# Two-layer attention backbone on Trainium2: reading gated attention back without its last pair, cutting the first output quarter inside the last attention unit, and adding residuals to partial sums

## The chip, the cores and the metric

The kernel runs on one core of a Trainium2 chip (trn2). The metric is device time in microseconds (us) of one execution, as the median of several runs. Beside it there is a hardware profile of one execution. Its engines are PE (TensorE matmul), PEld (weight load of TensorE), DVE (VectorE), ACT (ScalarE), POOL (GpSimd) and SP, the queue that issues nearly all DMAs.

## The reference

Two layers over 1024 latent tokens and 256 context tokens, width 1024. Layer 0 is windowed attention; the change lies wholly in the end of layer 1, multi-head latent attention, whose context output is not needed:

```
def attend(qn, qr, kn, kr, v):
    s = (einsum("bqhd,bkhd->bhqk", qn, kn) + einsum("bqhd,bkd->bhqk", qr, kr)) * scale
    p = softmax(s, axis=-1)
    return einsum("bhqk,bkhd->bqhd", p, v)
...
yx = (ox * silu(gx)) @ w_out                 # ox: 1024 tokens x 1024 channels, 16 heads of 64
x = x + gate_x[:, None] * yx                 # gate_x is folded into w_out by the kernel
return rms_norm(x, final_g)                  # y / sqrt(mean(y*y) + eps) * final_g
```

## The kernel before

**Attention.** The 16 heads are 8 pairs; each pair's 1024 queries are two halves of 512. That makes 16 units (`UnitB`), number `ui` = 2 * pair + half. A unit goes over `NT` = 10 chunks of 128 keys: `score` (L1820) makes the scores of two heads on PE, `exp` (L1830) takes their exponentials on ACT, an engine adds them up for the softmax's denominator (L1834 and L1836: POOL, but DVE in unit 15), and `PV` (L1843) multiplies by the values on PE, its result always in bank 7 of PSUM. `top` (L1786, L1792) finds the next unit's row maxima, `turn` and `shift` (L1800, L1804) bring them into its scores. `fin` (L1847) copies the PV result out and loads the gate; `fin2` (L1854, L1856) sums the denominator on PE and copies it out on ACT; `inv` (L1860, DVE) takes the reciprocal of a half of 256 tokens; `gate` (two POOL multiplications L1865 and a store L1867) writes gated attention to `og_d`, [pair, channel, token], in HBM. Units 0 to 13 are gated in chunk 0 of the unit two later; unit 14 inside unit 15 from chunk 5 on; unit 15 after the attention is over.

**Free PE slots.** After unit `ui`, PE makes the keys of the next pair (`make_K`) or, after units 3, 7 and 11, the values of the next four heads (`make_V`, five PSUM tiles in three banks, each copied out by ACT at L1732).

**The output weight** is multiplied by the gate and combined to seven 512x512 blocks of four k-slices each by `wo_pieces`, a generator that `wo_step` advances a few steps per unit, on POOL or on DVE. Every block is kept as two parts (a rounded `hi` on ACT and a rest `lo`, `split`, L281 and L282; on POOL L1880 and L1881). 18 of the 28 slices are written to `wb_d` in HBM and later read back by `wo_back` (L1886).

**The output product** (`out_sets`) takes 256 tokens at a time: four sets n = 0 to 3. The set's tokens are two rows of 128, its channels two halves, so it is a 2x2 block matrix a11, a12 / a21, a22; the 2x2 product takes seven block products instead of eight, in the order `WAY`: a11 with B11, a12 with B21, s2 with T2, s1 with T1, s4 with B22, s3 with T3, a22 with T4, where s1 = a21+a22, s2 = s1-a11, s4 = a12-s2, s3 = a11-a21. One block product is 12 matmuls (L286, L287, L288: hi by hi, lo by hi, hi by lo, for four k-slices). `fetch_raw(n)` loads the set's two rows from `og_d`, all eight pairs (a11 and a21 are pairs 0 to 3; a12 and a22 pairs 4 to 7; pair 7 is the last to come: sets 0 and 1 need unit 14, sets 2 and 3 unit 15). `sums` makes s1 to s4 on POOL; `all_cuts` splits the seven operands into hi and lo in a ring of six; five operands are ready ahead of the product.

After the products DVE adds up `ya` (row 0) and `yb` (row 1) from PSUM, POOL adds the residual rows `xa`, `xb`, ACT sums the squares (`square`, L2020), `tile_rstd` makes the norm's factor on POOL, `tile_out` scales and stores. For set 3 the last product, a22 with T4, is done in two halves of 256 columns.

**Order.** In this part each engine works its instructions off in the order of the code, and so does each DMA queue: an SP DMA that waits holds back all those behind it. Names in the profile: `arena_r` and `arena_f` are the two big buffers in which nearly everything lies, `PB` is PSUM, `small` holds the columns of the norm.

Of the kernel before, what the change touches and what calls it, by code (L numbers as in the profile page):

```python
# [11 lines left out]
F32 = mybir.dt.float32  # L12
# [205 lines left out]
def kernel(ctx: ExitStack, tc: tile.TileContext, t, out, dbg=None):  # L218
# [1739 lines left out]
    def fetch_raw(n):  # L1958
        for j in range(2):
            ts = slice((2 * n + j) * 128, (2 * n + j) * 128 + 128)  # L1960
            load(out=rawr[n % 2][j].bitcast(F32), in_=og_d[:, :, ts].rearrange("c p n -> p c n"))
# [16 lines left out]
    def sums(n):  # L1978
        (a11, a12), (a21, a22) = raw_parts(n)
        P = nc.gpsimd  # L1980
        ss[n] = s1, s2, s3, s4 = [shp(sr1.next(), 4, 128) for _ in range(4)]
        P.tensor_add(s1, a21, a22)
        yield
        P.tensor_sub(s2, s1, a11)
        yield
        P.tensor_sub(s4, a12, s2)
        yield
        P.tensor_sub(s3, a11, a21)
        yield

    def all_cuts():
        for n in range(4):
            (a11, a12), (a21, a22) = raw_parts(n)
            yield cut(a11, nc.vector if n else nc.gpsimd)
            yield cut(a12, nc.vector if n else nc.gpsimd)
            s1, s2, s3, s4 = ss[n]
# [25 lines left out]
    def out_sets(A, made, xs, u):  # L2022
# [7 lines left out]
        for n in range(4):  # L2030
# [4 lines left out]
            plus = sums(n + 1) if n < 3 else iter(())  # L2035
            for j in range(6 if last else 7):
                g = 7 * n + j
                ps = out_product(A.pop(0), WAY[j])
                if j < 4:
                    next(plus, None)  # L2040
# [5 lines left out]
                if n == 0 and j == 0:  # L2046
                    u.fin2(psd)
                if n == 0 and j < 2:
                    u.inv(j)
                    u.gate(256 * j, 256 * j + 256)  # L2050
                if n == 0 and j == 1:
                    wo_back("T4", 3)
# [14 lines left out]
                if j == 3:  # L2067
                    p5, u4 = ps, ur.next()
                    V.tensor_add(u4, ps, u2)
                if j == 4:  # L2070
                    V.tensor_add(ya[:, up], ps, u4)
                    at(g + 1, lambda ya=ya, xa=xa: P.tensor_add(ya[:, up], ya[:, up], xa[:, up]))
                    at(g + 1 if last else g + 2, lambda ya=ya, sa=sa: (square(ya, up, sa, 1), tile_rstd(sa)))
                    if not last:
                        for c in range(2):
                            at(g + 3, lambda ti=2 * n, ya=ya, sa=sa, c=c: tile_out(ti, ya, sa, c))
                if j == 5:
# [3 lines left out]
                    if last:  # L2081
                        V.tensor_add(yb[:, up], yb[:, up], xb[:, up])
                        P.tensor_add(u3, u3, xb[:, lo])
                        square(yb, up, sb, 1)
                        continue
# [11 lines left out]
        z = ur.next()  # L2097
        halves = [slice(256 * h, 256 * h + 256) for h in range(2)]
        for h, cs in enumerate(halves):
            ps = out_product(W, "T4", cs)  # L2100
            V.tensor_sub(yb[:, cs], u3[:, cs], ps)
            square(yb, cs, sb, 2 if h else 0)
            if h == 0:
                V.tensor_mul(z, yb[:, up], fg[:, up])
# [188 lines left out]
```

## Time and profile before

| what | value |
|---|---|
| median of 3 runs | 1485.5 us (1485.28 to 1487.9) |
| profiled execution | 1484.49 us, its span 1482.7 us |
| PE busy | 1454.4 us, 98% of the span |
| DVE, POOL, ACT busy | 76%, 59%, 50% |
| chain that ended last | PE 87%, DVE 5%, issue 2%, DMA 2%, ACT 2%, POOL 1% |
| granted clock of PE | 0.999 |

How to read it: the shares are means over stages that differ, so the end of the program is shown by stage. The work from the profile's 1260 us to its end, by stage (busy us of each engine, number of instructions, then clock, DMA share and GB/s; the stages are unit 11's end, units 12 to 14, unit 15, the output product, the end):

```profile
1260.00:1291.00 31.00, 30.08 (x222) 22.66 (x220) 24.76 (x26) 12.92 (x17) 30.15 (x16) 1.00 0.30 98
1291.00:1369.00 78.00, 78.00 (x570) 54.50 (x566) 53.91 (x76) 33.49 (x38) 74.33 (x37) 1.00 0.40 139
1369.00:1400.00 31.00, 27.16 (x163) 14.64 (x161) 21.65 (x16) 15.93 (x21) 18.56 (x13) 1.00 0.59 188
1400.00:1474.00 74.00, 73.61 (x335) 61.32 (x335) 57.37 (x61) 24.77 (x56) 57.41 (x57) 1.00 0.45 157
1474.00:1483.00 9.00, 0.05 (x1) 0.00 (x0) 3.78 (x9) 1.92 (x7) 1.05 (x2) 0.77 0.31 117
```

The columns are length, then PE, PEld, DVE, ACT and POOL. Times in the text, such as "at 1391.95", are us from the span's start.

### The profile page before, as it was taken

The page shows a single profiled execution, that of the slowest core. Times are in us where ns is not written, and L with a number is a line of the kernel's source. Part 1 is how long each engine was busy: PE and PEld are TensorE (multiplying, and loading weights), DVE is VectorE, ACT ScalarE, POOL GpSimd, SP SyncE. Part 2 cuts the span into 40 slices and gives each one's busy share as a digit, 9 for nine tenths or more (in the row PEclk, how much of TensorE's full clock was granted, in tenths as well). Part 3 has the DMA queues.
Part 4 walks back from the last instruction along what each step waited for, and adds up shares of the span by engine and source line. Part 5 has one row for each costly group of instructions (what it writes and reads, how often), then busy time and mean ns, then how long its engine had stood idle before and what let it go on. Part 6 is the DMA issues. An engine that isn't in the chain of part 4 may idle for free.

```text
span 1482.7 us, 25146 instructions
## 1 busy us (share of the span) xinstructions
PE 1454.4 (98%) x8988; PEld 1176.6 (79%) x8988; DVE 1128.9 (76%) x2064; ACT 746.2 (50%) x1419; POOL 870.4 (59%) x765
## 2 busy tenths in 40 slices
PE   7999999999999999999999999999999999999897
PEld 4888888888888888889888888766777767775586
DVE  4787789648778888878988777677777687776776
ACT  4421222259888878877554433443444434443432
POOL 2463366256464444456300240699999999999685
PEclk9999999999999999999999999999999999999999
DMA  9555644573343333338344566021312332325652
GB/s 337 171 173 170 212 155 164 181 251 108 122 141 121 104 100 100 94 95 263 95 120 119 172 224 204 15 64 44 103 47 74 102 118 89 104 88 183 223 174 100
DMA packets 152150, 204.90 MB, mean 138 GB/s; under 512 B 13388, under 2 KB 101068, under 8 KB 152024
## 3 DMA queue, kind: packets, MB, share of 16 engines
q1 hardware_dynamic: 147048, 196.63, 41.3%
q10 hardware_dynamic: 4976, 6.66, 1.3%
q8 instruction: 71, 1.16, 0.3%
q14 instruction: 55, 0.45, 0.1%
HBM read 143.46 MB, written 55.59 MB: 134 GB/s over the span
## 4 chain that ended last, share of the span: by engine, by line
PE 87%; DVE 5%; issue 2%; DMA 2%; ACT 2%; POOL 1%; SPq 0%; ACTq 0%; POOLq 0%; DVEq 0%
PE PB L286 14%; PE PB L287 14%; PE PB L288 14%; PE PB L1820 12%; PE PB L1843 8%; PE PB L738 5%; PE PB L1786 5%; PE PB L728 5%; PE PB L699 3%; PE PB L698 2%; PE PB L912 1%; DVE arena_r L282 1%; PE PB L1854 1%; PE PB L883 1%; PE PB L917 1%
## 5 line engine op out<-in xcount | busy, mean ns | idle before, releaser
L286 PE MATMUL PB<-arena_r 128*128 128x512 f32 (+2 forms) x1180 | 432.7, 367 | 2.0 <-DVE arena_f L1262 1.1
L287 PE MATMUL PB<-arena_r 128*128 128x512 f32 (+2 forms) x1180 | 427.0, 362 | 3.8 <-POOL arena_r L282 3.7
L288 PE MATMUL PB<-arena_r 128*128 128x512 f32 (+2 forms) x1180 | 426.4, 362 | 0.0
L1836 POOL TENSOR_TENSOR arena_f<-arena_f 128x1024 f32<-128x1024 f32 x120 | 292.8, 2440 | 9.4
L286 PEld LDWEIGHTS PB<-arena_r 128*128 128x128 f32 x1180 | 222.5, 189 | 47.2 <-issue 10.7
L287 PEld LDWEIGHTS PB<-arena_r 128*128 128x128 f32 x1180 | 222.6, 189 | 35.7 <-POOL arena_r L282 5.2
L288 PEld LDWEIGHTS PB<-arena_r 128*128 128x128 f32 x1180 | 222.5, 189 | 33.2
L1820 PE MATMUL PB<-arena_r 64*128 64x512 f32 (+1 forms) x1600 | 227.0, 395 | 0.0
L1830 ACT ACTIVATE arena_f<-PB 128x1024 f32<-128x1024 f32 x160 | 164.6, 1028 | 119.5 <-PE PB L1820 91.6
L1792 DVE TENSOR_REDUCE krF<-PB 128x1 f32<-128x512 f32 (+1 forms) x264 | 166.9, 678 | 50.6 <-PE PB L1786 50.6
L1820 PEld LDWEIGHTS PB<-arena_r 64*128 64x128 f32 (+1 forms) x1600 | 175.7, 185 | 16.1 <-issue 5.2
L705 DVE CUSTOM_DVE_ANT_0 arena_f<-PB,arena_f,small 128x256 f32<-128x256 f32 (+1 forms) x288 | 148.2, 525 | 51.0 <-PE PB L699 32.8
L281 ACT CAST arena_r<-PB 128x512 fp32r<-128x512 f32 (+2 forms) x207 | 115.4, 564 | 107.0 <-PE PB L288 68.3
L281 ACT CAST arena_r<-arena_f 128x512 fp32r<-128x512 f32 (+1 forms) x156 | 90.8, 612 | 133.7 <-PE PB L288 33.8
L282 DVE TENSOR_TENSOR arena_r<-PB,arena_r 128x512 fp32r<-128x512 f32 (+2 forms) x207 | 134.3, 661 | 26.7 <-ACT arena_r L281 26.0
L1843 PE MATMUL PB<-arena_f 128*64 128x512 f32 x640 | 146.4, 595 | 0.5 <-ACT arena_f L1830 0.5
L282 POOL TENSOR_TENSOR arena_r<-arena_f,arena_r 128x512 fp32r<-128x512 f32 (+1 forms) x48 | 67.5, 1427 | 105.2 <-ACT arena_r L281 105.0
L711 ACT ACTIVATE arena_f<-arena_f,small 128x640 f32<-128x640 f32 (+2 forms) x160 | 119.1, 745 | 15.5 <-DVE small L705 13.9
L508 DVE SCALAR_TENSOR_TENSOR arena_f<-arena_f,small 128x512 f32<-128x512 f32 x98 | 114.0, 1208 | 11.7 <-DMA arena_f<-ada_w 11.5
L738 PE MATMUL PB<-arena_r 128*128 128x512 f32 x336 | 118.9, 430 | 0.2 <-DVE arena_r L282 0.2
L282 DVE TENSOR_TENSOR arena_r<-arena_f,arena_r 128x512 fp32r<-128x512 f32 (+1 forms) x108 | 91.6, 872 | 27.6 <-ACT arena_r L281 24.9
L1786 PE MATMUL PB<-arena_r 64*128 64x512 f32 (+1 forms) x768 | 111.7, 355 | 0.1
(244 smaller groups left out, 2247.0 us busy)
## 6 DMA issues: line engine op xcount, KB each, us to landing
arena_f<-ada_w SPq DMA_DIRECT2D x96, 256.0 KB, 4.0
arena_r<-q_d SPq DMA_DIRECT2D x160, 128.0 KB, 2.8
arena_f<-a_w_in SPq DMA_DIRECT2D x40, 256.0 KB, 3.4
arena_f<-x_d SPq DMA_DIRECT2D x18, 512.0 KB, 4.8
arena_f<-b_w_in SPq DMA_DIRECT2D x36, 256.0 KB, 3.1
wb_d<-arena_r SPq DMA_DIRECT2D x18, 512.0 KB, 2.9
arena_r<-wb_d SPq DMA_DIRECT2D x18, 512.0 KB, 9.2
arena_f<-x SPq DMA_DIRECT2D x16, 512.0 KB, 5.8
```

The lines of the kernel that those rows point to most:

```text
L281: nc.scalar.copy(hi, src)
L282: (lo_eng or nc.vector).tensor_sub(lo, src, hi.bitcast(F32))
L286: nc.tensor.matmul(o, ah, bh, start=first, stop=False)
L287: nc.tensor.matmul(o, al, bh, start=False, stop=False)
L288: nc.tensor.matmul(o, ah, bl, start=False, stop=last)
L738: nc.tensor.matmul(self.pv, V[:, self.chunks[ci], self.g, :], PT[:, s], start=ci == 0 and s == 0, stop=ci == self.m - 1 and s == 1,)
L1786: nc.tensor.matmul(bank[:, o : o + n], self.q[r, s, bs], k[r, 0, n0 : n0 + n], start=s == 0, stop=s == 2)
L1792: nc.vector.reduce_max(self.mxp[:, e, b : b + 1, i], bank[:, 0:n], AX.X)
L1820: nc.tensor.matmul(PB[:, b + e, :], k[r, s, cs], q[r, sq], start=i == 0, stop=i == 4)
L1830: nc.scalar.activation(E, PB[:, b : b + 2, :], AF.Exp)
L1836: eng.tensor_add(acc, acc, E)
L1843: nc.tensor.matmul(PB[r, 7, :], Vq[:, c, h, :], E[:, e], start=c == 0, stop=c == NT - 1)
```

## The change

No matmul is added or taken away. Five things differ.

1. `fetch_raw` can load a range of pairs. For sets 0 and 1, pairs 0 to 6 are loaded in unit 14 (chunk 4), and pair 7 alone in unit 15, where all eight were loaded before.
2. In unit 15, right after unit 14's `fin2` (chunk 5), a11 of set 0 is split (ACT and POOL) and s3 of set 0 is made on POOL, both ahead of unit 14's `gate`; s3 of set 1 follows the gate. `sums` makes the same four sums in the order s3, s2 = a22-s3, s1, s4. a12 of set 0 is split behind the unit's last exponential, its `lo` on DVE instead of POOL. Unit 15's own `fin2`, `inv` and `gate` come one product later.
3. The weight slices are read back in four groups in units 12 to 14 instead of one group of ten in unit 14 and two in unit 15.
4. After unit 11 `wo_step` makes one step on DVE instead of three; the rest moves back, so that the last piece (L1932 and its split) is made on DVE in unit 13.
5. Set 3: the residuals `xb` and `xa` take partial sums before the last products come (u2 and p5 into `xb`; `xa` into u4), `xa` and `z` take ya and yb times `fg`, ACT scales row 0 of the last set (`scale_out`), and the POOL addition to u3 between the last two products is gone.

The diff, cut to its core:

```diff
+    def fetch_raw(n, c0=0, c1=8):
...
-        P.tensor_add(s1, a21, a22)
-        P.tensor_sub(s2, s1, a11)
-        P.tensor_sub(s4, a12, s2)
-        P.tensor_sub(s3, a11, a21)
+        P.tensor_sub(s3, a11, a21)
+        P.tensor_sub(s2, a22, s3)
+        P.tensor_add(s1, a21, a22)
+        P.tensor_sub(s4, a12, s2)
...
-            yield cut(a12, nc.vector if n else nc.gpsimd)
+            yield cut(a12, nc.vector)
...
+    def scale_out(ti, y, st, cs):
+        nc.scalar.activation(y[:, cs], y[:, cs], AF.Copy, scale=st[:, 3:4])
+        load(out=out[ti * 128 : ti * 128 + 128, cs], in_=y[:, cs])
...
+                if last:
+                    if j == 2:
+                        at(g + 1, lambda ya=ya: V.tensor_mul(xa[:, lo], ya[:, lo], fg[:, lo]))
+                        P.tensor_add(xb[:, lo], u2, xb[:, lo])
+                    if j == 3:
+                        V.tensor_add(xb[:, up], ps, xb[:, up])
+                        P.tensor_add(u4, u4, xa[:, up])
+                        V.tensor_add(xb[:, up], u2, xb[:, up])
+                    if j == 4:
+                        V.tensor_add(ya[:, up], ps, u4)
+                        square(ya, up, sa, 1)
+                        tile_rstd(sa)
+                        V.tensor_mul(xa[:, up], ya[:, up], fg[:, up])
+                        scale_out(6, xa, sa, lo)
+                    if j == 5:
+                        V.tensor_add(yb[:, up], ps, xb[:, up])
+                        square(yb, up, sb, 1)
+                        V.tensor_add(xb[:, lo], ps, xb[:, lo])
+                        z = ur.next()
+                        P.tensor_mul(z, yb[:, up], fg[:, up])
+                        scale_out(6, xa, sa, up)
+                    continue
...
-                    if last:
-                        V.tensor_add(yb[:, up], yb[:, up], xb[:, up])
-                        P.tensor_add(u3, u3, xb[:, lo])
...
-            V.tensor_sub(yb[:, cs], u3[:, cs], ps)
+            V.tensor_sub(yb[:, cs], xb[:, cs], ps)
...
+    backs = {
+        (12, 4): [("B11", 2), ("B22", 2), ("T1", 2), ("T2", 2)],
+        (13, 2): [("B21", 2), ("B11", 3), ("B22", 3)],
+        (13, NT): [("T1", 3), ("T2", 3), ("B21", 3)],
+        (14, 2): [("T3", 0), ("T3", 1)],
+    }
...
                 pu.fin2(PB[:, 2, :])
+                made, plus = all_cuts(), [sums(n) for n in range(4)]
+                A = [next(made)]
+                next(plus[0])
                 u.PV(0, 5)
                 pu.inv(0)
                 pu.gate(0, 256)
-                fetch_raw(0)
+                fetch_raw(0, 7)
                 pu.inv(1)
                 pu.gate(256, 512)
-                fetch_raw(1)
-                made, plus = all_cuts(), sums(0)
-                A = []
+                fetch_raw(1, 7)
+                next(plus[1])
...
+            if ui == 14 and c == 4:
+                for n in range(2):
+                    fetch_raw(n, 0, 7)
...
-                    wo_step(3 if ui % 4 == 3 else 1, nc.vector)
+                    wo_step(3 if ui % 4 == 3 and ui < 11 else 1, nc.vector)
```

How it moves instructions at the places that the prediction speaks of. First ACT after unit 11: L281 is the `hi` of a weight slice, L1732 the copies of the values' PSUM tiles, L1856 and L1847 the copies of `fin2` and `fin`.

```order
 L1830 ACTIVATE arena_f<-PB 128x1024 x10
 L1856 COPY arena_f<-PB 128x512
-L281 CAST arena_r<-arena_f 128x512 x2
+L281 CAST arena_r<-arena_f 128x512
 L1732 COPY arena_f<-PB 128x512 x5
 L1847 COPY arena_f<-PB 128x512
```

One of the two casts ahead of the copies is gone from here (it stands two units later, behind unit 13's `fin2`).

POOL in unit 15, before: the 128x512 pair L1865 is unit 13's gate, the two 128x256 pairs unit 14's; L1982 to L1988 are s1, s2, s4, s3; L282 is a `lo`, first of a11, then of a12.

```order
L1865 TENSOR_TENSOR arena_f<-arena_f 128x512
L1865 TENSOR_TENSOR arena_f<-arena_f,arena_r 128x256
L1865 TENSOR_TENSOR arena_f<-arena_f 128x256
L1865 TENSOR_TENSOR arena_f<-arena_f,arena_r 128x256
L1865 TENSOR_TENSOR arena_f<-arena_f 128x256
L1982 TENSOR_TENSOR arena_f<-arena_r 128x512
L1984 TENSOR_TENSOR arena_f<-arena_f,arena_r 128x512
L282 TENSOR_TENSOR arena_r<-arena_r 128x512
L1986 TENSOR_TENSOR arena_f<-arena_r,arena_f 128x512
L1988 TENSOR_TENSOR arena_f<-arena_r 128x512
L282 TENSOR_TENSOR arena_r<-arena_r 128x512
```

The same place of the changed kernel, whose lines L1983 to L1989 are s3, s2, s1, s4:

```order
L1865 TENSOR_TENSOR arena_f<-arena_f 128x512
L282 TENSOR_TENSOR arena_r<-arena_r 128x512
L1983 TENSOR_TENSOR arena_f<-arena_r 128x512
L1865 TENSOR_TENSOR arena_f<-arena_f,arena_r 128x256
L1865 TENSOR_TENSOR arena_f<-arena_f 128x256
L1865 TENSOR_TENSOR arena_f<-arena_f,arena_r 128x256
L1865 TENSOR_TENSOR arena_f<-arena_f 128x256
L1983 TENSOR_TENSOR arena_f<-arena_r 128x512
L1985 TENSOR_TENSOR arena_f<-arena_r,arena_f 128x512
L1987 TENSOR_TENSOR arena_f<-arena_r 128x512
L1989 TENSOR_TENSOR arena_f<-arena_r,arena_f 128x512
```

The split of a11 and one s3 now stand ahead of unit 14's gate, and a12's `lo` has left POOL.

ACT in the same unit, as one piece of the difference: L1830 are the ten exponentials, L281 with `arena_r<-arena_r` the `hi` of a11 and a12.

```order
 L1830 ACTIVATE arena_f<-PB 128x1024 x5
 L1856 COPY arena_f<-PB 128x512
-L1830 ACTIVATE arena_f<-PB 128x1024 x3
 L281 CAST arena_r<-arena_r 128x512
-L1830 ACTIVATE arena_f<-PB 128x1024
+L1830 ACTIVATE arena_f<-PB 128x1024 x5
 L281 CAST arena_r<-arena_r 128x512
-L1830 ACTIVATE arena_f<-PB 128x1024
```

The last two exponentials no longer stand behind a cast.

DVE at the very end, before: L2071 adds the fifth product, L2079 and L2080 the sixth, L2082 the residual, L2101 the two halves of the seventh, L2112 scales.

```order
L2071 TENSOR_TENSOR arena_f<-PB,arena_f 128x512
L2079 TENSOR_TENSOR arena_f<-PB,arena_f 128x512
L2080 TENSOR_TENSOR arena_f<-PB,arena_f 128x512
L2082 TENSOR_TENSOR arena_f<-arena_f 128x512
L2101 TENSOR_TENSOR arena_f<-arena_f,PB 128x256
L2104 TENSOR_TENSOR arena_f<-arena_f 128x512
L2016 SCALAR_TENSOR_TENSOR arena_f<-arena_f,small 128x512
L2101 TENSOR_TENSOR arena_f<-arena_f,PB 128x256
```

And now (L2083 adds the fifth product, L2089 and L2091 the sixth, L2120 the two halves of the seventh):

```order
L2073 TENSOR_TENSOR arena_f<-PB,arena_f 128x512
L2079 TENSOR_TENSOR arena_f<-PB,arena_f 128x512
L2081 TENSOR_TENSOR arena_f<-arena_f 128x512
L2083 TENSOR_TENSOR arena_f<-PB,arena_f 128x512
L2086 TENSOR_TENSOR arena_f<-arena_f 128x512
L2089 TENSOR_TENSOR arena_f<-PB,arena_f 128x512
L2091 TENSOR_TENSOR arena_f<-PB,arena_f 128x512
L2120 TENSOR_TENSOR arena_f<-arena_f,PB 128x256 x2
```

Residual additions and multiplications by `fg` moved ahead of the sixth product; nothing stands between the halves of the seventh.

More of the change, by code (lines that the diff above doesn't have):

```diff
@@ L2034, in out_sets @@
             last = n == 3
-            plus = sums(n + 1) if n < 3 else iter(())
             for j in range(6 if last else 7):
@@ L2209 @@
                 wo_back("T3", k)
-            A += [next(made) for _ in range(2)]
+            A.append(next(made))
         u.fin()
+    A += [next(made) for _ in range(3)]
     xs = fetch_x(0)
```

71 lines of the change are left out of this document (30 added, 41 removed).

## Prediction

> **What bounds the kernel now.** I read the whole page first, then what PE waited for from 1260 us on, the chain that ended last, and the timelines of the engines at each wait.
>
> ```profile
> span 1482.7 us, 25146 instructions
> ...
> PE 1454.4 (98%) x8988; PEld 1176.6 (79%) x8988; DVE 1128.9 (76%) x2064; ACT 746.2 (50%) x1419; POOL 870.4 (59%) x765
> ...
> PE PB L287 <- POOL arena_r L282: 3.7, 2, 2.9
> PE PB L286 <- ACT arena_f L1732: 0.9, 1, 0.9
> PE PB L1843 <- ACT arena_f L1830: 0.5, 2, 0.4
> ```
>
> PE is busy 98%, and no matmul is removed. Time can come only from PE's waits and from what follows its last matmul. The last three rows (waited for: us, times, longest) are all of PE's waits in the changed part. In PE's timeline (start, us, [idle before, releaser]):
>
> ```profile
> 1283.36 0.39 PE L286 MATMUL PB<-arena_r 128*128 128x256 f32 x1 [0.92 <-ACT arena_f L1732]
> ...
> 1376.18 4.46 PE L1843 MATMUL PB<-arena_f 128*64 128x512 f32 x20
> 1380.57 6.06 PE L1820 MATMUL PB<-arena_r 64*128 64x512 f32 x50
> 1386.56 2.79 PE L1843 MATMUL PB<-arena_f 128*64 128x512 f32 x12
> ...
> 1391.95 0.50 PE L286 MATMUL PB<-arena_r 128*128 128x512 f32 x1
> 1395.32 0.50 PE L287 MATMUL PB<-arena_r 128*128 128x512 f32 x1 [2.87 <-POOL arena_r L282]
> ...
> 1400.39 0.50 PE L287 MATMUL PB<-arena_r 128*128 128x512 f32 x1 [0.86 <-POOL arena_r L282]
> ...
> 1468.29 0.39 PE L286 MATMUL PB<-arena_r 128*128 128x512 f32 x1
> ...
> 1470.79 0.39 PE L288 MATMUL PB<-arena_r 128*128 128x512 f32 x1
> 1471.01 0.28 PE L286 MATMUL PB<-arena_r 128*128 128x256 f32 x1
> ...
> 1473.77 0.28 PE L288 MATMUL PB<-arena_r 128*128 128x256 f32 x1
> ```
>
> The first two products wait for the `lo` of a11 (2.87) and of a12 (0.86); from then on PE runs at 1471.01 - 1468.29 = 2.72 us per product and ends at 1474.05. Why the `lo` is late:
>
> ```profile
> 1387.92 0.62 ACT L281 CAST arena_r<-arena_r 128x512 fp32r<-128x512 f32 x1 [2.53 <-DMA arena_r<-og_d]
> ...
> 1380.63 0.75 POOL L1865 TENSOR_TENSOR arena_f<-arena_f 128x256 f32<-128x256 f32 x1 [5.55 <-DVE arena_f L1860]
> ...
> 1389.55 2.29 POOL L1982 TENSOR_TENSOR arena_f<-arena_r 128x512 f32<-128x512 f32 x1 [6.57 <-DMA arena_r<-og_d]
> ...
> 1396.93 1.73 POOL L1988 TENSOR_TENSOR arena_f<-arena_r 128x512 f32<-128x512 f32 x1
> ...
> 1381.40 0.32 SPq L1867 DMA_DIRECT2D og_d<-arena_f  x1
> 1383.80 1.00 SPq L1961 DMA_DIRECT2D arena_r<-og_d  x2
> ...
> arena_r<-og_d SPq DMA_DIRECT2D x8, 512.0 KB, 4.8
> ...
> arena_r<-qr_d SPq DMA_DIRECT2D x6, 64.0 KB, 4.7
> ```
>
> POOL multiplies the gate, SP stores, waits 2.40 us (1381.40 to 1383.80), loads 512 KB rows back (4.8 us to landing), and only then do ACT and POOL begin on a11, though only pair 7 is new. The cast also holds the exponentials of chunks 8 and 9 behind it on ACT.
>
> **Part 1, the exponentials: 1.00 us.** Without the cast, chunk 8's exponential starts when its scores end (40th of the 50 matmuls from 1380.57), at 1385.4, about 3 us before that cast is done. The last 20 PV matmuls then run through like those from 1376.18, whose pitch is 1380.57 - 1376.18 = 4.39, and end at 1390.95 instead of 1391.95. Bounds 0 and 1.00; I take 1.00.
>
> **Part 2, a11 and a12: 2.87 + 0.86 = 3.73 us.** a11's hi and lo are made in the 5.55 us that POOL idles, behind `fin2`'s copy:
>
> ```profile
> 1376.47 0.59 ACT L1856 COPY arena_f<-PB 128x512 f32<-128x512 f32 x1
> ...
> 1394.73 6.15 DVE L282 TENSOR_TENSOR arena_r<-arena_f,arena_r 128x512 fp32r<-128x512 f32 x4 [1.80 <-ACT arena_r L281]
> ```
>
> Cast 1377.06 to 1377.68, POOL's lo and s3 (1.73 each, as L1988) to 1379.4 and 1381.1: the first product has its operand 10 us early. The cost: unit 14's gate stands behind them; its two instructions (0.75 each) end at 1382.6 instead of 1381.38, and the store goes 1.2 us later, the small loads at 1382.65 + 2.40 = 1385.05 and half a us after. How fast 64 KB land alone, no row shows. Bounds: at once, or 4.7 us like the 64 KB loads that queue behind larger ones; I take the late end. Then a12 is there at 1389.75, its cast ends at 1390.4, and DVE (at most 6.15 / 4 = 1.54 per lo) has it at 1391.9; it is needed after the first product, 1390.95 + 2.72 = 1393.67. a22 lands at 1390.25; s2 takes POOL to 1392.0, cast and lo to 1394.2, needed after the second product and the `fin2` behind it, past 1396.4. s1 and s4 follow 1.73 apart on POOL and are needed 2.72 apart. So neither wait comes back: bounds 0 and 3.73, I take 3.73. The cover is 1.8 us for a12; beyond that each us of landing costs one.
>
> The Trainium skill speaks against the cut (DMA: Bandwidth & Descriptors, Rules for kernel authors): many small transfers should be coalesced, since under 64 KB mostly overhead is paid. By the fit of that page (Anatomy of one DMA, 2.0 us and the bytes over 436 GB/s) I estimate 2.15 us for 64 KB and 3.2 for 512 KB, so the overhead is real, but the piece would come sooner than in my sum; the 4.8 us row is above the fit.
>
> **Part 3, unit 15's own gate, the early loads and the readbacks: 0.** Unit 15's `fin2` comes one product later, the products 1.00 + 3.73 = 4.73 us earlier: the gate comes only 4.73 - 2.72 = 2.0 us earlier, and with it the load of set 2, which POOL's first sum of that set wants 4.73 earlier.
>
> ```profile
> 1409.31 1.03 SPq L1961 DMA_DIRECT2D arena_r<-og_d  x2
> ...
> 1418.46 1.74 POOL L1982 TENSOR_TENSOR arena_f<-arena_r 128x512 f32<-128x512 f32 x1
> ```
>
> Before, the second of the two was issued by 1409.8, landed about 1414.6 (4.8), and was used at 1418.46: of 3.9 us of slack 2.7 go, 1.2 stay. The sum's result is a split operand that PE takes two products or more after it, so even 1.2 us too late would be covered. The twelve readbacks move up one to three units on SP's queue; behind them stand the next units' query loads, wanted a unit later, and the gate's store and loads of unit 15 now have two readbacks fewer ahead. Of PE's waits in this part (the three rows at the top) none is for a DMA. Bounds: 0 and the slips that the rivals price; I take 0.
>
> **Part 4, the step after unit 11: 0.92 us.**
>
> ```profile
> 1279.23 2.89 DVE L1914 TENSOR_TENSOR arena_f<-arena_f,arena_r 128x512 f32<-128x512 f32 x1
> ...
> 1282.20 0.62 ACT L281 CAST arena_r<-arena_f 128x512 fp32r<-128x512 f32 x1 [7.61 <-DVE arena_f L1914]
> ...
> 1338.81 1.41 DVE L1804 TENSOR_TENSOR arena_r<-PB,ident 4x512 fp32r<-4x512 f32 x2 [4.68 <-PE PB L1800]
> ```
>
> ACT's copies of the values' tiles stand behind a cast that waits for L1914; PE runs out of banks and waits 0.92. Both go: bounds 0 and 0.92, I take 0.92. The moved pair of DVE and its cast land in unit 13's idle 4.68 us; at 2.89 + 0.62 + 1.54 = 5.05 they can make `shift` 0.4 us late, and the scores that use it come after 20 PV matmuls (4.39): 0. The rest of the shift exchanges one weight step for another of like size on POOL.
>
> **Part 5, the end: 2.31 us.**
>
> ```profile
> 1468.49 0.69 DVE L2071 TENSOR_TENSOR arena_f<-PB,arena_f 128x512 f32<-128x512 f32 x1 [1.84 <-PE PB L288]
> 1471.21 0.69 DVE L2079 TENSOR_TENSOR arena_f<-PB,arena_f 128x512 f32<-128x512 f32 x1 [2.03 <-PE PB L288]
> ...
> 1474.53 0.42 DVE L2101 TENSOR_TENSOR arena_f<-arena_f,PB 128x256 f32<-128x256 f32 x1 [1.17 <-POOL arena_f L2083]
> ...
> 1476.39 0.41 DVE L2101 TENSOR_TENSOR arena_f<-arena_f,PB 128x256 f32<-128x256 f32 x1
> ...
> 1479.04 0.33 SPq L2114 DMA_DIRECT2D out<-arena_f  x1
> ```
>
> The last matmul ends at 1474.05, but its half is subtracted only at 1476.39: DVE first waits for POOL's L2083, then does row 0's scaling. In the changed order DVE has only two additions (0.69 each) after the sixth product, 1471.21 to 1472.6, then the first half at once, then the second 0.03 us after its matmul, as L2079 at 1471.21 follows the matmul that ends at 1470.79 + 0.39 = 1471.18: 1474.08. From there to the last issue it is 1479.04 - 1476.39 = 2.65 as before. Gain 1476.39 - 1474.08 = 2.31. ACT must be free by 1474.6: row 0's square, POOL's factor and the scaling end by about 1472.3 (I allow 3.8 us from L2071's start), then a square, a scaling and the first half's square (at most 0.7 each, by the 0.62 of the 128x512 cast above): 1474.4. Bounds: 0, if that chain slips 2.3 us, and 2.31; I take 2.31.
>
> POOL now adds `xa` to u4 between two DVE additions. The Trainium skill (GPSIMD Engine Reference, Engine selection) would put such additions on VectorE, GpSimd being about twice as slow with two inputs; the rows 1.73 and 0.69 agree. If that step comes 1 us late, ACT's square slips by 0.4 and the sum below is 7.6 instead of 8.0.
>
> **Sum.** 1.00 + 3.73 + 0.92 + 2.31 = 7.96 us. The span goes from 1482.7 to 1474.7; the profiled execution from 1484.49 to 1476.5; its time is 1.0 below the median of 1485.5, so for the median I forecast 1477.5. A change under 0.2% (3 us) can't be told from none.
>
> **Rivals.**
> - *The end keeps its length.* POOL and DVE depend on each other in a loop through the sets:
>
> ```profile
> 1425.82 0.55 POOL L2012 TENSOR_TENSOR small<-small 128x1 f32<-128x1 f32 x1
> ...
> 1445.28 0.55 POOL L2012 TENSOR_TENSOR small<-small 128x1 f32<-128x1 f32 x1
> ```
>
> The loop takes 19.46 us, PE's set 7 x 2.72 = 19.04; it falls back 0.42 per set. The 1.84 us that DVE still waits for PE in the last set speaks against; added work there for. Loss 2.31: 1479.8.
> - *The wait moves.* The pieces land over 1.8 us later than my late bound, and the second and third product wait instead. With 3.73 lost: 1481.2. For: gate and store are later. Against: 64 KB have an eighth of the row's bytes.
> - *Both*, or the change does not do what it says: 7.96 - 2.31 - 3.73 = 1.9 left, 1483.6: no change that shows.
> - *Slower.* a11's split and s3 stand in front of the gate on POOL. If the early loads landed late, the gate, the store and all that follows would slip.
>
> ```profile
> 1349.16 6.37 SPq L1886 DMA_DIRECT2D arena_r<-wb_d  x10
> ...
> arena_r<-wb_d SPq DMA_DIRECT2D x18, 512.0 KB, 9.2
> ```
>
> Ten loads issued from 1349.16 took a median 9.2 us; four early ones from about 1352 should land by 1363, the cast wants them at 1377.06. A slip of d costs d - 1.8; over 3 us slower needs d above 12.8, a landing after 1389.9: 1488.5 and more.
>
> **Chances.** Forecast 0.74, end kept 0.09, wait moved 0.08, both 0.06, slower 0.03. Faster by over 0.2%: 0.91; within 0.06; slower 0.03. Range: below by 1.7 for the median's own spread (the first run lay 2.4 above it), 1475.8; above to the moved wait, 1481.3. The forecast's own is 1475.8 to 1479.
>
> **What would show it.** Right: no PE wait on POOL's L282; unit 15's PV without a gap; five copies after unit 11 without PE waiting; the last subtraction within 0.1 us of the last matmul. Wrong: PE waiting for a `lo` of a12 or s2, or DVE for POOL or ACT for `scale_out` behind the sixth product.

## The result and the profile after

| | median | lowest to highest | profiled execution, span |
|---|---|---|---|
| before | 1485.61 us (6 runs) | 1485.08 to 1487.9 | 1484.49, 1482.7 |
| after | 1476.82 us (6 runs) | 1475.99 to 1477.2 | 1476.32, 1474.5 |

The ratio is 0.9938, with a 95% interval of 0.9925 to 0.9951. The forecast was 1477.5. The head of the changed kernel's page, and what PE waited for between 1255 and 1480 us:

```profile
span 1474.5 us, 25163 instructions
...
PE 1453.1 (99%) x8988; PEld 1179.2 (80%) x8988; DVE 1129.9 (77%) x2065; ACT 747.3 (51%) x1421; POOL 872.8 (59%) x765
...
PE PB L287 <- DVE arena_r L282: 0.4, 1, 0.4
```

The number of matmuls has stayed (8988) and their busy time nearly so (1454.4 and 1453.1 us); the five waits of before in this part (3.7, 0.9 and 0.5 us) are gone, and there is a new one of 0.4. PE's timeline of the changed kernel, at the places of the rows of before:

```profile
1277.30 0.39 PE L286 MATMUL PB<-arena_r 128*128 128x256 f32 x1
...
1384.72 4.51 PE L1843 MATMUL PB<-arena_f 128*64 128x512 f32 x20
1389.16 0.50 PE L286 MATMUL PB<-arena_r 128*128 128x512 f32 x1
1389.50 0.39 PE L287 MATMUL PB<-arena_r 128*128 128x512 f32 x1
1389.73 0.40 PE L288 MATMUL PB<-arena_r 128*128 128x512 f32 x1
...
1392.02 0.39 PE L286 MATMUL PB<-arena_r 128*128 128x512 f32 x1
1392.82 0.50 PE L287 MATMUL PB<-arena_r 128*128 128x512 f32 x1 [0.41 <-DVE arena_r L282]
...
1464.71 0.28 PE L286 MATMUL PB<-arena_r 128*128 128x256 f32 x1
...
1467.46 0.28 PE L288 MATMUL PB<-arena_r 128*128 128x256 f32 x1
```

The 20 last PV matmuls now stand in one row, with no gap ahead of the first product, and a11's `lo` costs nothing: L287 follows L286 0.34 us later (1389.50 - 1389.16), where before it followed 3.37 us later (1395.32 - 1391.95). Inside a product the next matmul starts 0.23 later (1389.73 - 1389.50).

Spans of single profiles can't be compared to a tenth: the first value matmul after unit 11 (1277.30 here) starts between 1276.8 and 1279.6 us in the fourteen profiles of this study, though the kernels differ only behind it. So I measure from that matmul. The stages, each from the starts (and the end of the last matmul) in the timelines: **V** from the first value matmul to unit 12's first score; **PV** from the last 20 PV matmuls of unit 15 to the first product; **C** from there to the first half of the last product; **D** from the last matmul's end to the last subtraction; **E** from there to SP's last issue; **all** from the first value matmul to that issue. The rows from the third on are the experiments. They ran in three rounds, and the median of before was 1485.13, 1485.67 and 1485.91 us beside them, so medians of different rounds compare to about 0.8 us. The median of readback late is over three runs; a fourth took 1607.68 us at a granted clock of 0.851 and is left out.

| kernel | V | PV | C | D | E | all | median us |
|---|---|---|---|---|---|---|---|
| before | 8.56 | 5.39 | 79.06 | 2.34 | 2.65 | 201.18 | 1485.61 |
| after | 7.37 | 4.44 | 75.55 | 0.04 | 2.87 | 193.35 | 1476.82 |
| after, again | 7.38 | 4.44 | 76.01 | 0.03 | 2.66 | 193.68 | 1476.99 |
| three steps | 8.48 | 4.44 | 75.41 | 0.04 | 2.94 | 194.49 | 1477.00 |
| five steps | 15.96 | 4.44 | 75.75 | 0.03 | 2.66 | 201.90 | 1485.28 |
| old end | 7.38 | 4.44 | 76.05 | 2.34 | 2.65 | 196.03 | 1479.00 |
| whole rows | 7.38 | 5.67 | 80.39 | 0.03 | 3.02 | 199.66 | 1483.13 |
| gate first | 7.38 | 4.44 | 77.06 | 0.04 | 2.66 | 194.75 | 1479.08 |
| four pairs late | 7.38 | 4.44 | 76.04 | 0.04 | 2.66 | 193.71 | 1477.32 |
| readback late | 7.38 | 4.44 | 76.10 | 0.04 | 2.66 | 193.70 | 1477.22 |
| a12 lo on POOL | 7.38 | 4.44 | 75.93 | 0.03 | 2.66 | 193.56 | 1476.50 |
| s3 not ahead | 7.38 | 4.45 | 75.03 | 0.03 | 2.84 | 192.89 | 1477.18 |
| long stall (of before) | 8.49 | 5.81 | 82.62 | 2.34 | 2.65 | 205.07 | 1488.69 |
| short end | 7.38 | 4.44 | 74.81 | 0.03 | 2.66 | 192.44 | 1476.33 |

From before to after, "all" loses 7.83 us: 1.19 in V, 0.95 in PV, 3.51 in C, 2.30 in D, -0.22 in E, and 0.10 in the rest. The sum in the prediction was 7.96.

### The profile page after: what moved, and what is told of

Same layout as the page of the kernel before. It is cut to its first block, busy times and chain, and to the rows that moved or that the text cites. A ratio compares the mean times of both kernels' runs of the same rounds, so it can differ in the third digit from the quotient of the medians.

```text
span 1474.5 us, 25163 instructions
## 1 busy us (share of the span) xinstructions
PE 1453.1 (99%) x8988; PEld 1179.2 (80%) x8988; DVE 1129.9 (77%) x2065; ACT 747.3 (51%) x1421; POOL 872.8 (59%) x765
## 5 line engine op out<-in xcount | busy, mean ns | idle before, releaser
L286 PE MATMUL PB<-arena_r 128*128 128x512 f32 (+2 forms) x1180 | 432.6, 367 | 1.1 <-DVE arena_f L1262 1.1
L287 PE MATMUL PB<-arena_r 128*128 128x512 f32 (+2 forms) x1180 | 426.9, 362 | 0.5 <-DVE arena_r L282 0.4
L1836 POOL TENSOR_TENSOR arena_f<-arena_f 128x1024 f32<-128x1024 f32 x120 | 293.0, 2441 | 9.4
L286 PEld LDWEIGHTS PB<-arena_r 128*128 128x128 f32 x1180 | 222.5, 189 | 46.0 <-issue 10.6
L287 PEld LDWEIGHTS PB<-arena_r 128*128 128x128 f32 x1180 | 222.6, 189 | 32.4 <-DVE arena_r L282 0.8
L1820 PE MATMUL PB<-arena_r 64*128 64x512 f32 (+1 forms) x1600 | 229.3, 394 | 0.0
L1830 ACT ACTIVATE arena_f<-PB 128x1024 f32<-128x1024 f32 x160 | 164.6, 1028 | 119.0 <-PE PB L1820 90.4
L1820 PEld LDWEIGHTS PB<-arena_r 64*128 64x128 f32 (+1 forms) x1600 | 179.9, 185 | 13.7 <-issue 5.2
L281 ACT CAST arena_r<-PB 128x512 fp32r<-128x512 f32 (+2 forms) x207 | 115.3, 563 | 106.5 <-PE PB L288 68.3
L282 DVE TENSOR_TENSOR arena_r<-PB,arena_r 128x512 fp32r<-128x512 f32 (+2 forms) x207 | 134.3, 661 | 25.9 <-ACT arena_r L281 25.1
L281 ACT CAST arena_r<-arena_f 128x512 fp32r<-128x512 f32 (+1 forms) x156 | 90.7, 613 | 124.6 <-PE PB L288 33.7
L282 POOL TENSOR_TENSOR arena_r<-arena_f,arena_r 128x512 fp32r<-128x512 f32 (+1 forms) x48 | 67.6, 1428 | 104.7 <-ACT arena_r L281 82.6
L1786 PE MATMUL PB<-arena_r 64*128 64x512 f32 (+1 forms) x768 | 113.9, 355 | 0.1
L728 PE MATMUL PB<-ident,arena_f 128*128 128x128 f32 x672 | 108.7, 272 | 0.1
```

What stands on the lines that cost most here:

```text
L281: nc.scalar.copy(hi, src)
L282: (lo_eng or nc.vector).tensor_sub(lo, src, hi.bitcast(F32))
L286: nc.tensor.matmul(o, ah, bh, start=first, stop=False)
L287: nc.tensor.matmul(o, al, bh, start=False, stop=False)
L1820: nc.tensor.matmul(PB[:, b + e, :], k[r, s, cs], q[r, sq], start=i == 0, stop=i == 4)
L1830: nc.scalar.activation(E, PB[:, b : b + 2, :], AF.Exp)
```

## The experiments

The changed kernel run again, as a base for the others:

> The changed kernel again, as a control. Of the 8.2 us between the two spans, 0.56 had been gained before the first matmul of the values after unit 11 (1277.86 before, 1277.30 now), where nothing was changed. If that is chance, this run's start of that matmul scatters by about 0.6 us and its span is 1474.5 +- 0.8; all stage lengths behind it repeat within 0.1 us. If it is a real effect of the change (rival), the matmul starts at 1277.3 again in every run of it.

1476.99 us, ratio 0.9943 (0.9928 to 0.9958). C is 0.46 longer than in the first profile, where I had expected 0.1 at most: at the fourth slice of T4 PE waits for a readback.

```profile
1410.75 0.50 PE L286 MATMUL PB<-arena_r 128*128 128x512 f32 x1 [0.29 <-DMA arena_r<-wb_d]
...
1400.61 5.23 SPq L1867 DMA_DIRECT2D og_d<-arena_f  x2
1405.89 0.88 SPq L1886 DMA_DIRECT2D arena_r<-wb_d  x1
```

The readback stands behind the two stores of unit 15's gate on SP; the second store waited for POOL, and PE wanted the slice already 4.4 us after its issue. Such a wait (0.2 to 0.8) is in 6 of the 9 other profiles with the changed order of unit 15.

**Undoing one part each.** Part 5, the old code of the last set:

> The changed kernel with the old end of the last set (residuals added after the products, POOL's addition to u3 between the sixth and the seventh product). Theory: the subtraction of the last half again starts 2.3 us after PE's last matmul, and the span is 2.1 to 2.3 us longer than the control's. Rival (the end is set by the loop of POOL and DVE through the sets, so the order in the last set matters little): under 1 us longer.

```diff
-            V.tensor_sub(yb[:, cs], xb[:, cs], ps)
+            V.tensor_sub(yb[:, cs], u3[:, cs], ps)
```
(and with it the whole block `if last:` of the change). 1479.00 us, ratio 0.9959 (0.9945 to 0.9973). D is 2.34 again, to the hundredth, and "all" 2.35 longer than in the run beside it. The rows of DVE show the old gap and the old order:

```profile
1469.12 0.42 DVE L2105 TENSOR_TENSOR arena_f<-arena_f,PB 128x256 f32<-128x256 f32 x1 [1.17 <-POOL arena_f L2087]
1469.46 0.68 DVE L2108 TENSOR_TENSOR arena_f<-arena_f 128x512 f32<-128x512 f32 x1
...
1470.98 0.41 DVE L2105 TENSOR_TENSOR arena_f<-arena_f,PB 128x256 f32<-128x256 f32 x1
```

Parts 1 and 2, whole rows of `og_d` loaded in unit 15, a11 and a12 split and the sums made where they were:

> The changed kernel with all eight pairs loaded in unit 15, a11 split after that, the old order of the sums and a12's lo on POOL; readbacks, weight steps and the end stay changed. Theory: the waits for a11 and a12 (about 2.9 and 0.9) and the two for the exponentials return, the stretch from unit 15's last PV start to the first matmul of the last half product is about 4.4 us longer, and so is the span. Rival (the early readbacks or the end made much of the gain): under 2.5 us longer.

```diff
-                A = [next(made)]
-                next(plus[0])
...
-                fetch_raw(0, 7)
+                fetch_raw(0)
...
-                for n in range(2):
-                    fetch_raw(n, 0, 7)
```

1483.13 us, ratio 0.9986 (0.9976 to 0.9995): 6.14 above the changed kernel, and "all" 5.98 above it, more than the 4.73 of Parts 1 and 2 and the 4.4 that I expected. The waits of before are back, and something besides. PE's timeline, and PE's clock in one stretch (length, then PE, PEld, DVE, ACT, POOL, clock, DMA share and GB/s):

```profile
1390.93 0.50 PE L286 MATMUL PB<-arena_r 128*128 128x512 f32 x1
1394.32 0.59 PE L287 MATMUL PB<-arena_r 128*128 128x512 f32 x1 [2.88 <-POOL arena_r L282]
1394.71 0.63 PE L288 MATMUL PB<-arena_r 128*128 128x512 f32 x1
1395.14 0.63 PE L286 MATMUL PB<-arena_r 128*128 128x512 f32 x1
...
1398.07 0.39 PE L287 MATMUL PB<-arena_r 128*128 128x512 f32 x1
...
1394.00:1398.00 4.00, 3.68 (x9) 2.91 (x10) 3.86 (x3) 1.64 (x4) 4.00 (x4) 0.57 1.01 377
```

After a wait of 2.88 us the matmuls follow each other 0.43 us apart instead of 0.23, until 1398.07: the granted clock is 0.57 over that stretch. Eight such intervals cost 8 x 0.20 = 1.6 us. In the one profile of before, a wait of 2.87 at the same place was not followed by this.

Is that the stall's doing? The kernel before, with the first sum of set 0 made three times on POOL, so that PE waits longer:

> The kernel before with s1 of set 0 made three times on POOL (the same sum again), so that PE's wait for a11 grows from 2.9 to about 6.5 to 7.5 us. In one run with whole rows (wait 2.88) PE's matmuls after the wait ran at a pitch of 0.43 us instead of 0.23 for 3.8 us; in the run of before (wait 2.87) not. Theory (a wait of about 3 us is at the edge of what lets PE's clock drop, and a longer one drops it always): the matmuls after the long wait start at a pitch of 0.43 in this profile, the granted clock of that stretch is under 0.9, and the time is longer than before by the added wait of 3.6 to 4.6 us and 1.5 to 2 us more. Rival (the slow matmuls of that run had another cause): pitch 0.23, longer by the added wait alone.

```diff
-        P.tensor_add(s1, a21, a22)
+        for _ in range(3 if n == 0 else 1):
+            P.tensor_add(s1, a21, a22)
```

1488.69 us, ratio to before 1.0022 (1.0012 to 1.0032): 3.0 us slower, "all" 3.9 longer. The wait grew to 5.55 us, not to the 6.5 to 7.5 that I expected.

```profile
1398.89 0.80 PE L287 MATMUL PB<-arena_r 128*128 128x512 f32 x1 [5.55 <-POOL arena_r L282]
...
1399.00:1403.00 4.00, 4.00 (x10) 3.17 (x11) 3.73 (x4) 1.73 (x3) 4.00 (x3) 0.50 1.04 414
1404.00:1408.00 4.00, 4.00 (x19) 2.82 (x16) 3.10 (x3) 1.89 (x4) 3.04 (x4) 1.00 0.79 315
```

After a wait of 5.55 the clock is 0.50 until about 1403.3, then 1.00. So a pause of this length costs itself and some 2 us of half speed behind it. The Trainium skill states this (TensorE: Matmul & The Clock Gate, What's actually happening): the clock is halved after an idle window of about 3.4 us, and the window runs freely. The pause of 5.55 us agrees with it. The two of 2.88 and 2.87 (3.39 and 3.37 from start to start) lie just under that figure, and one of them was followed by half speed all the same. That the window runs freely might be why its twin was not; two profiles do not show it.

Part 4, three steps on DVE after unit 11 again, and then five:

> The changed kernel with three weight steps on DVE after unit 11 again. Theory (each part has its own place, the parts add up): the stretch from the first value matmul to the next unit's first score goes from 7.37 back to 8.56 us, with a PE wait of 0.9 us for ACT's copy, and the span is 1.2 us longer than the control's. Rival (the later waits take it up): the wait returns but the span is within 0.4 us of the control's, because what follows waits less.

> Changed kernel, but five steps of the output weight on DVE after unit 11 (one in the changed kernel, three before): three casts stand ahead of the copies of the values' tiles on ACT. Theory of Part 4 (copies behind a cast that waits for DVE cost PE time): the third cast comes one lo (1.54) and one DVE pair (2.89) later than the second, so PE waits 0.86 + 4.4 = about 5.3 us before the copies; from the first value matmul to the next score 8.48 + 4.4 = 12.9 us against 7.37; time 1477 + 5.5 = 1482.5 us. Rival (the wait does not reach the end, as the run with three steps took 1477.0 against 1477.0): time 1477 to 1478 us, with the wait in the profile or without.

```diff
-                    wo_step(3 if ui % 4 == 3 and ui < 11 else 1, nc.vector)
+                    wo_step(3 if ui % 4 == 3 else 1, nc.vector)
...
+                    wo_step(5 if ui == 11 else 3 if ui % 4 == 3 else 1, nc.vector)
```

Three steps: 1477.00 us, 0.0 from the changed kernel's 1476.99. The times alone would say that the wait never reached the end. The profile says otherwise: the wait is back (0.86), V is 8.48, and "all" is 0.8 to 1.1 longer; but this execution's first value matmul was at 1276.82, 0.5 to 1.2 us earlier than in the two of the changed kernel, and four runs of each kernel scatter by as much. Five steps settle it: 1485.28 us, 8.3 above the changed kernel, and "all" 8.2 to 8.6 above it. ACT's and PE's rows:

```profile
1281.22 0.62 ACT L281 CAST arena_r<-arena_f 128x512 fp32r<-128x512 f32 x1 [7.61 <-DVE arena_f L1914]
1286.65 0.62 ACT L281 CAST arena_r<-arena_f 128x512 fp32r<-128x512 f32 x1 [4.81 <-DMA wb_d<-arena_r]
...
1287.80 0.58 PE L286 MATMUL PB<-arena_r 128*128 128x256 f32 x1 [6.33 <-ACT arena_f L1732]
...
1288.00:1292.00 4.00, 4.00 (x19) 4.00 (x20) 0.46 (x1) 1.31 (x3) 0.35 (x1) 0.50 0.67 211
```

PE's wait reaches the end in full, and the rival is out. It is longer than the 5.3 us that I expected, because the third cast waits for the store of an earlier slice, not for DVE alone, and half speed follows again: 0.21 us between matmuls instead of 0.12 up to 1292.24, about 1.9 us.

The parts add up. In "all", undoing Part 5 costs 2.35, Parts 1 and 2 (undone only together) 5.98, Part 4 0.81: 9.14 us. Less the 1.6 of half speed in the profile of whole rows that is 7.5, and 7.50 lie between this base and the profile of before.

**What of the reading back matters.** Unit 14's gate ahead of a11's split; four pairs late instead of one; and the weight readbacks in one late group:

> The changed kernel with a11's split and the first s3 behind unit 14's gate on POOL instead of ahead of it. Theory (the order on POOL has slack on both sides): store and small load come 1.2 us earlier or the same, since the gate still waits for DVE's reciprocal; a11's lo is there by 1387, before the first product at 1389.2; PE waits within 0.3 us of the control's. Rival (the early split is what made the gain): the first product waits for a11 again, over 0.5 us.

> Changed kernel, but pairs 0 to 3 of sets 0 and 1 are loaded in unit 14 and pairs 4 to 7 in unit 15 (256 KB rows late instead of 64 KB). Theory (a11 early is what counts, the size of the late piece does not): the rows land between the 2.0 us seen for 64 KB and the 4.8 us seen for 512 KB, about 3.2; a12's lo stands behind DVE's last additions anyway, s2 starts up to 1.2 us later on POOL. First product to last half 75.5 to 76.5 us, as in the changed kernel (75.55, 76.01); 1477 us. Rival (the cut to the last pair brings it): the larger rows bring the waits of a12 or s2 back, 1 to 3.7 us: stage 77 to 79.5, 1478 to 1480.7 us.

> Changed kernel, but the ten readbacks of weight slices in one group in unit 14 (chunk 1) and the first two of T3 in unit 15 (chunk 0), as before the change. Theory (Part 3: where the readbacks stand costs nothing): no new PE wait, the stage lengths of the changed kernel (4.44 and 75.5 to 76.0), 1477 us. Rival (the groups were spread because the early loads of pairs 0 to 6 stand behind them on SP's queue): the early loads land late enough that a11's cast waits, unit 14's gate behind it slips, and PE waits before the second or third product: 1478 to 1481 us.

```diff
# gate first
-                A = [next(made)]
-                next(plus[0])
...
                 fetch_raw(1, 7)
+                A = [next(made)]
+                next(plus[0])
# four pairs late
-                fetch_raw(0, 7)
+                fetch_raw(0, 4)
# readback late
-        (12, 4): [("B11", 2), ("B22", 2), ("T1", 2), ("T2", 2)],
...
+        (14, 1): [(n, k) for n, k in away if n not in ("T3", "T4")],
+        (15, 0): [("T3", 0), ("T3", 1)],
```

Gate first: 1479.08 us, 0.9963 (0.9948 to 0.9978), C 1.0 to 1.5 longer, with PE waits of 1.14 (a12's `lo`) and 0.5 (the slice). Neither expectation came true: the first product does not wait for a11 (PV stays 4.44), and the time is lost all the same, at the second product; the cause is under "The new wait". Four pairs late: 1477.32, 0.9947 (0.9932 to 0.9962); the 256 KB rows landed in 3.5 us, the same stages as the changed kernel. Readback late: 1477.22, 0.9946 (0.9931 to 0.9961), the stages unchanged, with the same two small waits (0.30 and 0.36) as the changed kernel has. So it counts that pairs 0 to 3 are there early (whole rows, which also puts back the order of the sums, against four pairs late), and that a11's split does not fall behind the gate; that just one pair is left over does not, and neither does the spreading of the readbacks. How fast the late piece lands:

```profile
arena_r<-og_d SPq DMA_DIRECT2D x4, 64.0 KB, 2.0
...
arena_r<-og_d SPq DMA_DIRECT2D x4, 256.0 KB, 3.5
```

The first row is of the changed kernel, the second of the one with four pairs late.

**The new wait.** a12's `lo` on POOL, behind s2 and ahead of s1 and s4, instead of DVE; and s3 of set 1 no longer ahead on POOL:

> The changed kernel with the lo of a12 of set 0 on POOL, right behind s2 and ahead of s1 and s4. In the changed kernel DVE takes 9.56 us for its last five additions of the exponentials (1.91 each; 1.23 to 1.29 each before, where POOL stood still), and a12's lo behind them holds PE up by 0.24 to 0.41 us. Theory (DVE, slowed while POOL makes the sums, is what is late, not the DMA or the cast): the PE wait at the second product goes away, and the time from the first product to the third shrinks by about 0.5 us. Rival (the small load or ACT's cast is late): the wait stays, now on POOL.

> The changed kernel without POOL's s3 of set 1 in unit 15 (made in the output product instead), so that POOL has 2.3 us less work beside DVE's last five additions. Theory (DVE is slowed by POOL's work at the same time): the five additions take 0.6 to 0.9 us less than 9.56 and the PE wait at the second product (0.24 to 0.41) is gone. Rival (the additions are slow for another reason, the reads of the exponentials or ACT's writes): 9.5 us again, the wait stays. Under either, the span changes by under 0.6 us.

```diff
# a12 lo on POOL
-            yield cut(a12, nc.vector)
+            yield cut(a12, nc.vector if n else nc.gpsimd)
# s3 not ahead
-                if n < 3 and 0 < n + j < n + 4:
+                if n < 3 and j < 4:
...
                 fetch_raw(1, 7)
-                next(plus[1])
```

a12 lo on POOL: 1476.50 us (2 runs), 0.9943 (0.9923 to 0.9963). The wait for `lo` is gone, and all that it gave is taken by the slice of T4: PE waits 0.78 there, C 75.93. s3 not ahead: 1477.18 (2 runs), 0.9948 (0.9928 to 0.9968); in its profile neither wait is left and C is 75.03. DVE's last five additions for the denominator, in the kernels after, s3 not ahead and gate first, in this order:

```profile
1381.51 9.56 DVE L1836 TENSOR_TENSOR arena_f<-arena_f 128x1024 f32<-128x1024 f32 x5
1390.99 1.77 DVE L282 TENSOR_TENSOR arena_r<-arena_r 128x512 fp32r<-128x512 f32 x1
...
1382.29 8.67 DVE L1836 TENSOR_TENSOR arena_f<-arena_f 128x1024 f32<-128x1024 f32 x5
...
1381.74 10.55 DVE L1836 TENSOR_TENSOR arena_f<-arena_f 128x1024 f32<-128x1024 f32 x5 [0.33 <-ACT arena_f L1830]
```

The same five instructions take 9.56, 8.67 and 10.55 us, and PE waits 0.41, 0 and 1.14 for the `lo` behind them. They are longer the more POOL does beside them: its sums in these stretches are

```profile
1383.30 2.26 POOL L1983 TENSOR_TENSOR arena_f<-arena_r 128x512 f32<-128x512 f32 x1
...
1385.96 1.71 POOL L1985 TENSOR_TENSOR arena_f<-arena_r,arena_f 128x512 f32<-128x512 f32 x1 [1.84 <-DMA arena_r<-og_d]
...
1382.26 2.28 POOL L282 TENSOR_TENSOR arena_r<-arena_r 128x512 fp32r<-128x512 f32 x1
1384.49 4.48 POOL L1983 TENSOR_TENSOR arena_f<-arena_r 128x512 f32<-128x512 f32 x2
```

from 1383.30 on in the changed kernel, from 1385.96 on without the early s3, and from 1382.26 on with the gate first.

**A version with what the traces left.** a12's `lo` on POOL; the `hi` half of the late T4 slice read back ahead of the gate store; one addition moved behind the fifth product's; row 0's second scaling on DVE between the two last halves:

> Changed kernel with what the traces left: a12's lo of set 0 on POOL behind s2; the hi half of T4's last weight slice read back with the first three, ahead of unit 15's gate store on SP, the lo half where it was; in the last set the second addition of u2 to xb behind the fifth product's addition on DVE; row 0's second scaling on DVE between the two last halves instead of ACT. Theory: the waits of 0.24 to 0.41 (a12's lo) and 0.26 to 0.8 (weight slice) go, first product to last half 75.0 to 75.3 us (75.55 and 76.01 in the changed kernel); last subtraction to last issue 2.65 (2.66 and 2.87): 0.5 to 0.9 us less, 1476.2 us. Rivals: POOL's lo comes late or the sums slip: stage 75.5 or more, 1477 us; DVE's scaling delays the last subtraction by up to 0.4: 1476.6 us.

```diff
+    load(out=WB["T4"][3][:, 0].bitcast(F32), in_=away["T4", 3][:, 0])
...
+            if h == 0:
+                V.tensor_scalar_mul(xa[:, up], xa[:, up], sa[:, 3:4])
+                load(out=out[768:896, up], in_=xa[:, up])
```

1476.33 us (5 runs, 1475.66 to 1477.24), 0.9938 (0.9926 to 0.9951). PE has no wait left after 1255 us, C is 74.81, E 2.66, and "all" 0.9 to 1.2 us shorter than in the two profiles of the changed kernel. It has the lowest median of all kernels, but the times alone (1476.82 and 1476.99 against 1476.33) do not separate it.

## Why the prediction was right

**Part 1, 1.00 us: right.** PV lost 0.95. Chunk 8's exponential does not stand behind a cast any more: ACT's five run in one row and the cast follows at their end.

```profile
1380.21 5.65 ACT L1830 ACTIVATE arena_f<-PB 128x1024 f32<-128x1024 f32 x5 [4.49 <-PE PB L1820]
1385.75 0.61 ACT L281 CAST arena_r<-arena_r 128x512 fp32r<-128x512 f32 x1
```

**Part 2, 3.73 us: right in size, by two errors of opposite sign.** First, I took the stall from the "idle before" of the rows. That idle counts from the modelled end of the matmul before, and the next matmul normally starts earlier than that (at 1389.50, where the one before ends at 1389.16 + 0.50). From start to start the two pauses were 3.37 and 1.35 us (the second from the first row below to 1400.39) where 0.34 is normal at these places: 3.03 + 1.01 = 4.04 us. Second, a12's `lo` was expected from DVE 0.95 us after the first product's start (1391.9 - 1390.95) and came after 3.60: it ran from 1390.99 to 1392.76 and was wanted 0.23 after 1392.02. The need was where I had put it, but DVE's additions, which I had not costed, took 9.56 us. The new pause is 1392.82 - 1392.02 - 0.23 = 0.57 us, and in sum 4.04 - 0.57 = 3.47, against 3.51 in C. The rows to read were there before the change:

```profile
1399.04 0.49 PE L286 MATMUL PB<-arena_r 128*128 128x512 f32 x1
...
1383.10 3.88 DVE L1836 TENSOR_TENSOR arena_f<-arena_f 128x1024 f32<-128x1024 f32 x3 [1.00 <-ACT arena_f L1830]
1389.49 1.23 DVE L1836 TENSOR_TENSOR arena_f<-arena_f 128x1024 f32<-128x1024 f32 x1 [2.50 <-ACT arena_f L1830]
1390.92 2.00 DVE L1836 TENSOR_TENSOR arena_f<-arena_f 128x1024 f32<-128x1024 f32 x1 [0.21 <-ACT arena_f L1830]
```

DVE's L1836 took 3.88 us for three while POOL stood still, and 2.00 for one that started inside POOL's first sum (1389.55 to 1391.84). The rival "the wait moves" thus came true in its mechanism, at 0.57 us, and through DVE, not through a late load: the loads came 2.0 us after their issue, where I had taken 4.7. On the loads the estimate from the Trainium skill (DMA: Bandwidth & Descriptors, Anatomy of one DMA), 2.15 us for 64 KB, was nearer than my late bound, and the trace agrees with it there; for 512 KB it gives 3.2 where the row has 4.8. The page states that fit for DMAs that GpSimd issues, and these come from SP.

**Part 3, 0 us: wrong by up to half a us in the changed kernel.** I priced the load of set 2 behind the gate's store, but not the weight slice that stands between them on the same queue: PE came 4.7 us earlier, the store only about two by the prediction's own working. The wait of 0.2 to 0.8 shows in most profiles; in the changed kernel it is 0 in one and 0.44 from start to start in the other (1410.75, 0.67 after the matmul before it, where 0.23 is normal). The readbacks moved forward do cost nothing, as the kernel with the late group showed. (The 9.2 us in the rival "Slower" are the median of all 18 readbacks from 1260 us on; the ten by themselves took 9.5.)

**Part 4, 0.92 us: right, a little small.** V lost 1.19, again more than the row's idle. The five copies wait only for PE now (0.85 before each after the first):

```profile
1279.03 0.59 ACT L1732 COPY arena_f<-PB 128x512 f32<-128x512 f32 x1 [5.01 <-PE PB L288]
1280.47 0.59 ACT L1732 COPY arena_f<-PB 128x512 f32<-128x512 f32 x1 [0.85 <-PE PB L288]
```

**Part 5, 2.31 us: right, minus 0.2.** D lost 2.30, and E grew by 0.22; the last subtraction starts 0.04 after the last matmul's end, and DVE waits for PE and for nothing else:

```profile
1461.77 1.72 DVE L2081 TENSOR_TENSOR arena_f<-arena_f 128x512 f32<-128x512 f32 x1
1463.42 0.68 DVE L2083 TENSOR_TENSOR arena_f<-PB,arena_f 128x512 f32<-128x512 f32 x1
...
1467.78 0.42 DVE L2120 TENSOR_TENSOR arena_f<-arena_f,PB 128x256 f32<-128x256 f32 x1 [1.01 <-PE PB L288]
...
1470.65 0.33 SPq L2129 DMA_DIRECT2D out<-arena_f  x1
```

The 0.22 us given back in E is the chain that I named as a condition: L2081 takes 1.72 us beside POOL's addition, L2083 and with it row 0's square come late, and ACT is still at the first half's square when the second is subtracted:

```profile
1467.98 0.40 ACT L2025 ACTIVATE arena_f<-arena_f 128x256 bf16<-128x256 f32 x1
...
1468.51 0.42 ACT L2025 ACTIVATE arena_f<-arena_f 128x256 bf16<-128x256 f32 x1
```

The chain has no slack: with the new end, E is 2.84 to 3.02 in the profiles where PE lost no time to the weight slice and 2.66 in those where it did, and 2.66 also in the version with the shorter end, where PE lost none. The 1.73 us that I set beside DVE's 0.69 was read too high for POOL: that sum ran beside DVE's splits, and alone one takes 1.28.

**The median.** In "all", 7.96 forecast stands against 7.83 and 7.50. The medians fell by 8.8, about a us more: the profiled execution of before was 1.1 below its median, that of the changed kernel only 0.5. Half speed behind the old stall is the likely reason, and the profile of before would then be the exception among its executions. The three profiles with half speed have a mean granted clock of 0.996 or 0.997, all others 0.998 or 0.999 (that of before 0.999). Of 44 more executions of before, timed beside the experiments, 43 have 0.995 to 0.997 and one 0.999; all ten of the changed kernel have 0.999. It fits that the long stall cost 3.0 us in the median but 3.9 against the profile of before. But the mean does not say where the clock was low, and the one execution with 0.999 took 1484.63 us, not the least of its round; so how much of the us it explains is not shown. The prediction had no term for it. It took its sum from an execution that did not pay half speed, and that the gain in the median came out larger was not foreseen.

## What to carry to other kernels

When a producer on the critical path is slow only because its input is the last thing to arrive, split the input by arrival: what exists early goes early, and mind what the work that moves falls beside: here the order on POOL cost 1.0 to 1.5 us, the size of the late piece nothing. Cost a stall from start to start of the matmuls, and a moved step on an engine with the durations that it has while its neighbours are busy, its neighbours' included. Where runs scatter by as much as the effect, enlarge the suspected cost until the time shows it, and read small effects from a fixed point inside the profile.

## What the hardware showed that I had not expected

- DVE's addition of two 128x1024 tiles took 1.29 us with POOL standing still (3.88 / 3) and 1.73 to 2.11 on average with POOL adding beside it (8.67 / 5 to 10.55 / 5), while POOL's 128x512 sums went from 1.28 to 2.26. In the kernel before, an addition that had started 0.06 us ahead of POOL's sum took 1.23 and the sum 2.29; the next one, started inside that sum, took 2.00. The Trainium skill (SBUF — State Buffer, Who interferes with whom) says that a VectorE instruction with two SBUF inputs contends with a GpSimd instruction that reads SBUF. In the same page's Summary: rules for kernel authors, the Trainium skill adds that the second one to issue fully blocks until the first finishes. The rows agree: each time the later one is the longer, and over a stretch both lose.
- After PE waits of 5.55 and 6.33 us the granted clock was 0.50 for about 4.4 us; after 2.88 us it was low in one profile for 3.75 us, and after 2.87 us in another it was not.
- 64 KB landed 2.0 us after issue, 256 KB in 3.5 us, where the same kind of load of 512 KB took 4.8.
